# An encoder's second attention layer: five gate tiles instead of seven ahead of the first head group, three behind its operands, and values two token tiles to a PSUM bank

## The chip, the cores and the metric

One core of one Trainium2 chip runs the whole kernel in one launch. The metric is device microseconds of that core. A profiled execution of the same program gives the trace that all rows below come from; its times are counted from the first instruction.

## The reference, cut to what matters

A trunk of two layers over 512 tokens of width 1024. The first layer is a neighbourhood attention and is left alone by the change. The second is a multi-head latent attention of 16 heads, with low-rank queries (384) and keys and values (256), a rotary part of 32 per head, a part of 64 without rotation and values of 64. A gate silu(z) from the same input multiplies its output.

```python
def mixer_mla(xn, w_in, q_norm, w_qb, kv_norm, w_kvb, w_out):
    c_q, c_kv, k_rope, z = split(xn @ w_in, [384, 640, 672])
    q = (rmsnorm(c_q, q_norm) @ w_qb).reshape(B, S, H, 96)
    q_nope, q_pe = split(q, [64]);  q_pe = apply_rope(q_pe, cos, sin)
    kv = (rmsnorm(c_kv, kv_norm) @ w_kvb).reshape(B, S, H, 128)
    k_nope, v = split(kv, [64])
    k_pe = apply_rope(k_rope[:, :, None, :], cos, sin)      # one for all heads
    o = block_attention(concat(q_nope, q_pe), concat(k_nope, k_pe), v)
    return (o.reshape(B, S, H * 64) * silu(z)) @ w_out

for i in range(2):
    xn = rmsnorm(x, norm_g[i])
    h = x + (mixer_na if i == 0 else mixer_mla)(xn, ...)
    gate = sigmoid(rmsnorm(h, ple_norm[i]) @ ple_w_gate[i])
    x = h + gate * (p[i] @ ple_w_proj[i])
return rmsnorm(x, final_norm)
```

## The kernel before, in words

**Numbers.** Every float32 operand of a matmul is held as two tiles, a high part that TensorE takes directly and a low part with what the high part leaves out. A product is three matmuls: high by high, high by low, low by high. For a weight (`load_w`, L67) a DMA on SP brings `wraw`, ScalarE (ACT) copies it to `whi` (L76) and GpSimd (POOL) subtracts to `wlo` (L77). What comes out of PSUM is split in the same way (`split`, L81): ACT copies the high part (L83), VectorE (DVE) subtracts the low one (L85, or L87 with a scale). There are three buffers each of `wraw`, `whi` and `wlo`. PSUM has two banks under the tag `mm` for projections, two under `S` for scores, three under `T` for transposes and one under `O` for a head's output. A bank is 128 partitions by 512 float32.

**Order.** No order of instructions is written by hand across engines. A scheduler goes through the program at build time with a timeline of its own and sets, for each engine and for SP's queue, one fixed order; at run time each engine works its list from top to bottom and waits on semaphores. A tile that takes over a buffer waits until the last reader of the old one is done. `issue_after(i)` tells the scheduler to place nothing of the block ahead of instruction i.

**The second layer.** `mla_c` (L408) projects the layer's input (`x1h`, `x1l`, high and low) to c_q, c_kv and the rotary key, normalises each of four token tiles, rotates the key, transposes to columns (`cT`, high and low, L122) and collects the rotated keys in `slab_h` and `slab_l`. Twelve DMAs on SP (`move`, L89) copy these slabs into two sets of operand tiles: `qe`, `qo`, `ke`, `ko`, the queries and keys of the even and the odd head of a pair, each high and low.

`mla_heads` (L455) does the rest. It first issues the loads of the two rope tables, `rope_c` and `rope_s` (L459, L460). Eight z tiles of 128 gate columns follow one from the other: `z_phase` (L144) loads a weight, runs 24 matmuls of 512 columns into one `mm` bank and has ACT write silu of it to a `z` tile (L152). Seven of them (`NEARLY`, L30) are in the program before the first group, the eighth behind the first projection.

A `group(g)` (L477) serves two pairs, that is four heads: the rotary queries of all four (`psr`, 9 matmuls, copied to `xr` by ACT), the swap of halves `sw` (DVE, L484), the multiplications by the tables (L485 on DVE, L486 on POOL), their sum (L487, POOL), and its split into `rh` (ACT, L490) and `rl`; then the values of four token tiles, six matmuls of 256 columns each into a bank of their own, split by `v_split` (L174) into a tile `vt`; then the load of the weights for the part without rotation. `project(j)` (L507) makes the operands of pair j: nine matmuls for the queries and four evictions out of that bank, six for the keys and four more, and eight small moves of the rotary queries. `attend(j)` (L527) runs the two heads of a pair in `mla_head` (L547): for each of four query tiles three matmuls of scores in a bank `S`, the row maximum (DVE), the exponential `ex` with its sum (ACT), the reciprocal (DVE), the product (POOL), four transposes, the split into `pt_hi` (ACT) and `pt_lo` (DVE); then eight matmuls into the bank `O`. `combine` and `gated` (L157, L166) bring the two heads together in `u`, multiply by the pair's z tile and split into `oT`, whose four tiles are allocated ahead of `mla_heads` (L672). The loop at L535 to L545 strings these together.

## Time and profile before

| what | value |
|---|---|
| time, median of 3 runs | 691.67 us (691.35 to 691.88) |
| the profiled execution's own time | 690.26 us |
| its span, first to last instruction | 688.5 us |
| mean granted TensorE clock | 0.998 |
| first layer and `mla_c`, 0 to 402 | PE busy 391.7 of 402.0 us |
| `mla_heads`, 402 to 585 | PE busy 177.0, ACT 138.4, DVE 132.4, POOL 131.4 of 183.0 us |
| output projection and gate, 585 to the end | PE busy 95.7, POOL 49.4, ACT 42.6, DVE 38.3 of 103.5 us |
| HBM | 65.34 MB read, 8.39 MB written, 107 GB/s over the span |

PE is the TensorE matmul, PEld its weight load, which runs beside it, SP the engine that issues the DMAs. The borders 402 and 585 lie at the last transposes of `mla_c` and behind the last pair's attention. A granted clock of 1.00 is full speed. The busy time of PE is modelled at its ends, so that two waits that lie between back-to-back matmuls can be read better from starts of matmuls than from sums of busy time.

### The profile page before, as it was taken

Reading aid. Unit: us, or ns where it says so; the run is one execution under the profiler, and the core shown is the slowest. Engines: PE = TensorE matmul, PEld = TensorE weight load, DVE = VectorE, ACT = ScalarE, POOL = GpSimd, SP = SyncE. Lnnn points to the kernel's source line nnn. Section 1 sums busy time; section 2 is a strip of 40 time slices with the busy share of each in tenths; the row PEclk is TensorE's granted clock in tenths of the full one; section 3 lists DMA queues with packets and bytes.
Section 4 is the critical chain, followed back from the end, with each engine's and each line's share of the span. In section 5 each row is a group of like instructions: output and inputs, shape, how many; then the busy total and the mean of one; then the engine's idle time right before and its main releaser. Section 6 shows DMA issues by size and latency. Waiting matters only on the chain.

```text
span 688.5 us, 10118 instructions
## 1 busy us (share of the span) xinstructions
PE 664.4 (97%) x3580; PEld 566.9 (82%) x3580; DVE 356.3 (52%) x813; ACT 402.1 (58%) x799; POOL 396.7 (58%) x309
## 2 busy tenths in 40 slices
PE   5999999999999999999999998999999999999995
PEld 4789898998988888788899886787888777887885
DVE  4300364647737624633524503788988886055333
ACT  6722576666767562643443634878888878426433
POOL 1753557467575565853044634777789867658511
PEclk9999999999999999999999999999999999999999
DMA  8731423323223127544243344203121201584122
GB/s 324 234 121 62 133 86 104 105 72 97 85 92 108 40 97 301 167 130 135 89 104 107 107 121 116 81 23 93 24 70 37 86 1 68 191 308 154 61 77 92
DMA packets 28642, 77.53 MB, mean 113 GB/s; under 512 B 3632, under 2 KB 6704, under 8 KB 28592
## 3 DMA queue, kind: packets, MB, share of 16 engines
q1 hardware_dynamic: 28592, 76.89, 33.9%
q8 instruction: 28, 0.46, 0.3%
q14 instruction: 22, 0.18, 0.1%
HBM read 65.34 MB, written 8.39 MB: 107 GB/s over the span
## 4 chain that ended last, share of the span: by engine, by line
PE 86%; ACT 5%; DVE 4%; issue 2%; DMA 1%; POOL 1%; SPq 0%; POOLq 0%; DVEq 0%; ACTq 0%
PE ps_mm L96 63%; PE ps_S L96 9%; PE ps_T L122 5%; PE ps_O L96 4%; PE ps_O L335 2%; PE ps_T L323 1%; ACT ex L561 1%; ACT whi L76 1%; DMA x<-x 1%; PE ps_S L288 1%; PE ps_S L287 1%; DVE mx L559 1%; POOL wlo L77 0%; DVE mx L301 0%; ACT pt_hi L83 0%
## 5 line engine op out<-in xcount | busy, mean ns | idle before, releaser
L77 POOL TENSOR_TENSOR wlo<-wraw,whi 128x1024 fp32r<-128x1024 f32 (+3 forms) x96 | 218.3, 2287 | 118.5 <-ACT whi L76 68.4
L76 ACT ACTIVATE whi<-wraw 128x1024 fp32r<-128x1024 f32 (+4 forms) x100 | 97.9, 988 | 97.0 <-PE ps_mm L96 32.1
L563 POOL TENSOR_TENSOR ex<-ex,rc 128x512 f32<-128x512 f32 x64 | 66.2, 1048 | 20.7 <-DVE rc L562 13.9
L96 PE MATMUL ps_mm<-whi,hnT 128*128 128x512 f32 (+1 forms) x272 | 69.7, 377 | 0.0
L96 PEld LDWEIGHTS ps_mm<-whi,hnT 128*128 128x128 f32 x272 | 49.5, 188 | 9.5
L310 POOL TENSOR_TENSOR ex<-ex,rc 128x128 f32<-128x128 f32 (+1 forms) x64 | 34.3, 560 | 38.1 <-DVE rc L306 36.5
L559 DVE TENSOR_REDUCE mx<-ps_S 128x1 f32<-128x512 f32 x64 | 43.7, 685 | 15.3 <-PE ps_S L96 14.3
L96 PE MATMUL ps_mm<-xh,whi 128*128 128x512 f32 x192 | 50.9, 398 | 0.1
L96 PE MATMUL ps_mm<-xh,wlo 128*128 128x512 f32 x192 | 49.1, 391 | 0.0
L561 ACT ACTIVATE ex<-ps_S,mx 128x512 f32<-128x512 f32 x64 | 44.1, 689 | 8.2 <-DVE mx L559 6.7
L96 PE MATMUL ps_mm<-xl,whi 128*128 128x512 f32 x192 | 48.6, 392 | 0.0
L85 DVE TENSOR_TENSOR pt_lo<-ps_T,pt_hi 128x512 fp32r<-128x512 f32 x64 | 43.0, 679 | 5.0 <-ACT pt_hi L83 4.6
L305 ACT ACTIVATE ex<-ex,mx 128x128 f32<-128x128 f32 (+1 forms) x64 | 30.2, 473 | 22.0 <-DVE mx L301 21.6
L106 POOL TENSOR_TENSOR rs<-ss,half 128x1 f32<-128x1 f32 x24 | 13.0, 549 | 50.3 <-DVE ss L105 49.0
L96 PEld LDWEIGHTS ps_mm<-xl,whi 128*128 128x128 f32 x192 | 35.6, 188 | 7.3
L96 PEld LDWEIGHTS ps_mm<-xh,wlo 128*128 128x128 f32 x192 | 35.6, 188 | 7.0
L83 ACT ACTIVATE pt_hi<-ps_T 128x512 fp32r<-128x512 f32 x64 | 37.0, 597 | 7.6 <-PE ps_T L122 7.3
L96 PE MATMUL ps_mm<-wlo,hnT 128*128 128x512 f32 (+1 forms) x136 | 40.6, 379 | 0.0
L96 PEld LDWEIGHTS ps_mm<-xh,whi 128*128 128x128 f32 x192 | 34.5, 188 | 6.4 <-ACT z L152 0.4
L122 PE MATMUL ps_T<-ident,ex 128*128 128x128 f32 x256 | 36.3, 273 | 0.2 <-DVE pt_lo L85 0.2
L122 PEld LDWEIGHTS ps_T<-ident,ex 128*128 128x128 f32 x256 | 30.7, 141 | 6.8 <-issue 0.7
L85 DVE TENSOR_TENSOR vt<-ps_mm,vt 128x256 fp32r<-128x256 f32 x32 | 13.2, 415 | 44.3 <-ACT vt L83 44.0
(215 smaller groups left out, 1579.7 us busy)
## 6 DMA issues: line engine op xcount, KB each, us to landing
pe<-pe SPq DMA_DIRECT2D x32, 256.0 KB, 2.9
wraw<-na_qk SPq DMA_DIRECT2D x16, 512.0 KB, 3.4
wraw<-gate SPq DMA_DIRECT2D x16, 512.0 KB, 3.4
wraw<-na_z SPq DMA_DIRECT2D x8, 512.0 KB, 4.2
wraw<-na_v SPq DMA_DIRECT2D x8, 512.0 KB, 3.3
wraw<-na_o SPq DMA_DIRECT2D x8, 512.0 KB, 3.4
wraw<-mla_z SPq DMA_DIRECT2D x8, 512.0 KB, 4.2
wraw<-mla_o SPq DMA_DIRECT2D x8, 512.0 KB, 3.6
```

The costliest lines, as they stand in the source:

```text
L76: nc.scalar.activation(hi[:, c], raw[:, c], AF.Copy)
L77: (rest or nc.gpsimd).tensor_tensor(out=lo[:, c], in0=raw[:, c], in1=hi[:, c].bitcast(F32), op=ALU.subtract)
L83: nc.scalar.activation(hi, src, AF.Copy, scale=scale)
L85: nc.vector.tensor_tensor(out=lo, in0=src, in1=hi.bitcast(F32), op=ALU.subtract)
L96: last = nc.tensor.matmul(out, l, r, start=i == 0, stop=i == n - 1)
L122: self.nc.tensor.transpose(t[:, i * P:(i + 1) * P], b, self.ident)
L305: self.last_exp = nc.scalar.activation(e, e, AF.Exp, bias=mx[:, qt:qt + 1], accum_out=sm[:, qt:qt + 1])
L310: nc.gpsimd.tensor_tensor(out=e, in0=e, in1=rc[:, qt:qt + 1].to_broadcast([P, e.shape[1]]), op=ALU.mult)
L335: nc.tensor.matmul(O[:, o:o + w], vh[kt], s[:, c:c + w], start=n == 0, stop=n == 7, skip_group_check=True)
L559: nc.vector.reduce_max(mx[:, c], sp, axis=AX.X, negate=True)
L561: nc.scalar.activation(ex, sp, AF.Exp, bias=mx[:, c], accum_out=sm[:, c])
L563: nc.gpsimd.tensor_tensor(out=ex, in0=ex, in1=rc[:, c].to_broadcast([P, S]), op=ALU.mult)
```

## The change

Five things change, all in the second layer.

1. Five z tiles instead of seven (`NEARLY`) stand in the program ahead of the first group. The sixth comes behind `project(0)`. `attend(0)` may not be placed ahead of its last matmul (`last_mm`), and the seventh and eighth stand behind `attend(0)`.
2. These three are copied raw out of PSUM by DVE. Their silu are then done in place on ACT, the eighth first, each behind the one before it.
3. The values of two token tiles share a bank: twelve matmuls of 256 columns into the two halves, then one split of 512 columns into a `vt` tile of twice the width. There are four such tiles instead of eight.
4. The key-value weights and the weights of the queries without rotation are loaded, copied and split in two halves.
5. The second half of `oT` is allocated in the loop before `attend(3)` rather than at the start.

```diff
-NEARLY = 7
+NEARLY = 5
...
-            last = nc.tensor.matmul(out, l, r, start=i == 0, stop=i == n - 1)
+            last = self.last_mm = nc.tensor.matmul(out, l, r, start=i == 0, stop=i == n - 1)
...
-    def z_phase(self, wap, xT, js, after=None):
+    def z_phase(self, wap, xT, js, after=None, raw=False):
...
             z = self.zp.tile([P, S], F32, name="z", tag="z")
+            zs[j] = z
+            if raw:
+                self.nc.vector.tensor_copy(z, ps)
+                continue
             with self.tc.issue_after(after) if after is not None else nullcontext():
                 self.nc.scalar.activation(z, ps, AF.Silu)
-            zs[j] = z
...
-        src = ps.rearrange("p (g e c) -> p g e c", g=2, e=2)
-        hi = win(vt, 0, P, 0, [[256, 2], [192, 2], [1, 64]])
-        lo = win(vt, 0, P, 64, [[256, 2], [64, 2], [1, 64]])
+        g = ps.shape[1] // 128
+        src = ps.rearrange("p (g e c) -> p g e c", g=g, e=2)
+        hi = win(vt, 0, P, 0, [[256, g], [192, 2], [1, 64]])
+        lo = win(vt, 0, P, 64, [[256, g], [64, 2], [1, 64]])
...
-            wkv = self.load_w(a["mla_kv"][g], 1024)
+            wkv = self.load_w(a["mla_kv"][g], 1024, parts=2)
             vts = []
-            for t in range(NT):
+            for t0 in range(0, NT, 2):
                 ps = self.psum("mm")
...
-                self.mms(ps[:, :256], [(L(0, k), W(0, k)) for k in range(2)] + [(L(1, k), W(0, k)) for k in range(2)]
-                         + [(L(0, k), W(1, k)) for k in range(2)])
-                vt = pool.tile([P, S], F32R, name="vt", tag="vt", bufs=8)
-                self.v_split(vt, ps[:, :256])
-                vts.append(vt)
+                for t in (t0, t0 + 1):
...
+                    self.mms(ps[:, (t - t0) * 256:(t - t0 + 1) * 256],
+                             [(L(0, k), W(0, k)) for k in range(2)] + [(L(1, k), W(0, k)) for k in range(2)]
+                             + [(L(0, k), W(1, k)) for k in range(2)])
+                vt = pool.tile([P, 2 * S], F32R, name="vt", tag="vt", bufs=4)
+                self.v_split(vt, ps)
+                vts += [vt[:, :S], vt[:, S:]]
             V[g] = vts
-            W_[g] = wkv, self.load_w(a["mla_qn"][g], 768)
+            W_[g] = wkv, self.load_w(a["mla_qn"][g], 768, parts=2)
...
-        zs.update(self.z_phase(a["mla_z"], xT, range(NEARLY, 8)))
+        zs.update(self.z_phase(a["mla_z"], xT, [NEARLY], raw=True))
+        first = self.last_mm.ins
         for j in range(8):
             if j < 7 and j % 2 == 1:
                 group((j + 1) // 2)
-            attend(j)
+            if j == 3:
+                for s, n in enumerate("hl"):
+                    oT[s].append(self.bigtile(f"o1{n}1"))
+            with self.tc.issue_after(first) if j == 0 else nullcontext():
+                attend(j)
+            if j == 0:
+                zs.update(self.z_phase(a["mla_z"], xT, range(NEARLY + 1, 8), raw=True))
+                prev = None
+                for i in range(7, NEARLY - 1, -1):
+                    with self.tc.issue_after(prev) if prev is not None else nullcontext():
+                        prev = nc.scalar.activation(zs[i], zs[i], AF.Silu).ins
...
-                oT = ([self.bigtile(f"o1h{g}") for g in range(2)], [self.bigtile(f"o1l{g}") for g in range(2)])
+                oT = ([self.bigtile("o1h0")], [self.bigtile("o1l0")])
```

**The places where the order moves.** The first is the end of `mla_c` on PE, before the change. `ident,cn` are the transposes of the last token tile, `x1h` and `x1l` with a weight are z tiles.

```order
L122 MATMUL ps_T<-ident,cn 128x128 x6
L96 MATMUL ps_mm<-x1h_3092,wlo 128x512 x3
L96 MATMUL ps_mm<-x1h_3093,wlo 128x512 x4
L96 MATMUL ps_mm<-x1h_3092,whi 128x512 x4
L96 MATMUL ps_mm<-x1h_3093,whi 128x512 x4
L96 MATMUL ps_mm<-x1l_3094,whi 128x512 x4
L96 MATMUL ps_mm<-x1l_3095,whi 128x512 x4
```

The same place after the change; `cT` with a weight of 512 columns is the rotary projection of `group(0)`, with one of 256 columns its values.

```order
L122 MATMUL ps_T<-ident,cn 128x128 x6
L96 MATMUL ps_mm<-x1h_3092,wlo 128x512 x3
L96 MATMUL ps_mm<-x1h_3093,wlo 128x512 x4
L96 MATMUL ps_mm<-cT_3484,whi 128x512 x3
L96 MATMUL ps_mm<-cT_3485,whi 128x512 x3
L96 MATMUL ps_mm<-cT_3484,wlo 128x512 x3
L96 MATMUL ps_mm<-whi,cT_3484 128x256 x2
```

Where two z tiles stood behind the end of the z tile that surrounds the transposes, the first group now follows at once.

SP's queue at the same time, before the change, from the last move out of a slab to the first move of a rotary query:

```order
L90 DMA qo_3497<-slab_l 32x512
L75 DMA wraw<-mla_z 128x1024
L75 DMA wraw<-mla_qr 128x384
L459 DMA rope_c<-rope_c 128x512
L460 DMA rope_s<-rope_s 128x512
L75 DMA wraw<-mla_kv 128x1024
L75 DMA wraw<-mla_qn 128x768
L90 DMA qe_3486<-rh 32x512
```

And after it:

```order
L90 DMA qo_3497<-slab_l 32x512
L75 DMA wraw<-mla_z 128x1024
L75 DMA wraw<-mla_qr 128x384
L464 DMA rope_c<-rope_c 128x512
L465 DMA rope_s<-rope_s 128x512
L90 DMA qe_3486<-rh 32x512
```

The loads of the group's value and query weights have gone to places ahead of the moves; the two tables stand where they stood, behind all twelve moves.

The second place is DVE in `group(0)` and `project(0)`, before the change (`qe_3487`, `qo_3489`, `ke_3491`: low parts of the first pair's operands):

```order
L484 STREAM_SHUFFLE sw<-xr 128x512
L85 TENSOR_TENSOR vt<-ps_mm,vt 128x2x128
L485 TENSOR_TENSOR xr<-xr,rope_c 128x512
L85 TENSOR_TENSOR vt<-ps_mm,vt 128x2x128 x3
L87 SCALAR_TENSOR_TENSOR qe_3487<-ps_mm,qe_3486 64x512
L85 TENSOR_TENSOR ke_3491<-ps_mm,ke_3490 64x512
L87 SCALAR_TENSOR_TENSOR qo_3489<-ps_mm,qo_3488 64x512
```

After it:

```order
L489 STREAM_SHUFFLE sw<-xr 128x512
L85 TENSOR_TENSOR vt<-ps_mm,vt 128x4x128
L490 TENSOR_TENSOR xr<-xr,rope_c 128x512
L85 TENSOR_TENSOR vt<-ps_mm,vt 128x4x128
L87 SCALAR_TENSOR_TENSOR qe_3487<-ps_mm,qe_3486 64x512
L85 TENSOR_TENSOR ke_3491<-ps_mm,ke_3490 64x512
L87 SCALAR_TENSOR_TENSOR qo_3489<-ps_mm,qo_3488 64x512
L85 TENSOR_TENSOR ko_3493<-ps_mm,ko_3492 64x512
L154 COPY z<-ps_mm 128x512
```

Four splits of values have become two, one on either side of the multiplication by `rope_c`, and the raw copy of the sixth z tile stands behind the operands.

The third place is ACT. Before the change, from the last high parts of the first pair's operands to the start of its exponentials:

```order
L83 ACTIVATE ko_3492<-ps_mm 64x512
L76 ACTIVATE whi<-wraw 128x384
L152 ACTIVATE z<-ps_mm 128x512
L561 ACT_TABLE_LOAD
L561 ACTIVATE ex,sm<-ps_S,mx 128x512 x2
```

After it, in the second head of the first pair (`u` is the first head's output, `qe_3494` and `qo_3496` belong to the second pair):

```order
L579 ACTIVATE ex,sm<-ps_S,mx 128x512
L76 ACTIVATE whi<-wraw 128x512
L560 ACT_TABLE_LOAD
L560 ACTIVATE z<-z 128x512 x3
L76 ACTIVATE whi<-wraw 128x512
L83 ACTIVATE qe_3494<-ps_mm 64x512
L579 ACT_TABLE_LOAD
L579 ACTIVATE ex,sm<-ps_S,mx 128x512
L164 ACTIVATE u<-ps_O 64x512
L83 ACTIVATE pt_hi<-ps_T 128x4x128
L76 ACTIVATE whi<-wraw 128x384 x2
L83 ACTIVATE qo_3496<-ps_mm 64x512
```

Three silu with a table load on either side have come between two exponentials, where one silu with one table load stood ahead of the first.

2 lines of the change are left out of this document (1 added, 1 removed).

## The prediction, made before the changed kernel was run

> **What bounds the kernel now.** I read the page first, engine lines and then the chain that ended last.
>
> ```profile
> PE 664.4 (97%) x3580; PEld 566.9 (82%) x3580; DVE 356.3 (52%) x813; ACT 402.1 (58%) x799; POOL 396.7 (58%) x309
> PE 86%; ACT 5%; DVE 4%; issue 2%; DMA 1%; POOL 1%; SPq 0%; POOLq 0%; DVEq 0%; ACTq 0%
> ```
>
> TensorE is busy for 664.4 us of a span of 688.5, and 86% of the last chain is matmul. The change takes no matmul away, so it can only win idle time of PE, 24 us in all, or add to it. Where that idle time lies in the second layer is in the table by stretches (stretch; us of PE, PEld, DVE, ACT, POOL; clock; DMA):
>
> ```profile
> 402.00:412.90 10.90, 10.90 (x50) 9.03 (x49) 0.29 (x1) 3.38 (x5) 3.40 (x2) 1.00 0.57 149
> 412.90:425.60 12.70, 10.77 (x53) 7.96 (x52) 5.75 (x11) 6.56 (x12) 8.47 (x5) 1.00 0.53 148
> 425.60:438.80 13.20, 11.87 (x55) 9.69 (x55) 4.73 (x10) 7.88 (x15) 5.48 (x5) 1.00 0.12 35
> 438.80:468.80 30.00, 28.86 (x159) 24.23 (x159) 25.63 (x52) 24.08 (x55) 22.45 (x19) 1.00 0.19 52
> 468.80:585.00 116.20, 114.61 (x616) 94.46 (x617) 96.00 (x197) 96.53 (x212) 91.56 (x78) 1.00 0.18 55
> ```
>
> From 402.0 to 412.9 PE works through two z tiles without a pause. It idles 1.9 us in the first group and projection, 1.3 us at the start of the attention, 1.1 us more by 468.8 and 1.6 us in the whole remaining 116 us. So about 6 us are there to be won.
>
> **What the change moves: the first group to an earlier time.** Five z tiles instead of seven stand ahead of group(0). The timeline of PE at its borders (start, us, line, operands, count):
>
> ```profile
> 399.81 0.82 PE L122 MATMUL ps_T<-ident,cn 128*128 128x128 f32 x6
> 402.08 1.98 PE L96 MATMUL ps_mm<-x1h,whi 128*128 128x512 f32 x8
> 412.96 1.52 PE L96 MATMUL ps_mm<-cT,whi 128*128 128x512 f32 x6
> 425.64 2.06 PE L96 MATMUL ps_mm<-x1h,whi 128*128 128x512 f32 x8
> 82.82 5.47 PE ps_mm L96 x24
> ```
>
> The last row is a piece of the chain: 24 matmuls of 512 columns take 5.47 us when they run back to back, 0.228 us each. That is a z tile. Before, the sixth z tile begins at 402.08, group(0) at 412.96 and the eighth z tile at 425.64. After the change the same transposes (399.81) are followed by group(0) at 402.1, 10.9 us earlier, because everything ahead of it on PE stands as it did.
>
> What group(0) needs does not all move with it. Its rotation multiplies by the rope tables, and these stand in SP's queue behind the twelve moves out of slab_h and slab_l, in the old program and in the new one. SP's timeline, and from the views of both table tiles the time to landing:
>
> ```profile
> 402.30 0.60 SPq L90 DMA_DIRECT2D ke<-slab_h  x1
> 409.30 0.59 SPq L90 DMA_DIRECT2D qo<-slab_l  x1
> 411.07 1.50 SPq L459 DMA_DIRECT2D rope_c<-rope_c  x1
> 412.62 0.42 SPq L460 DMA_DIRECT2D rope_s<-rope_s  x1
> ...
> DMA to landing us min/median/max: 4.5/4.5/4.5
> ...
> DMA to landing us min/median/max: 3.6/3.6/3.6
> ```
>
> The moves start when the last slab_h is written and take SP until 409.9 (first and last of twelve shown). rope_c lands at 411.07 + 4.5 = 415.6, rope_s at 416.2. Before, that was just early enough:
>
> ```profile
> 402.00 0.28 ACT L83 ACTIVATE slab_h<-ps_T 128x128 fp32r<-128x128 f32 x1 [0.79 <-DVE cT L85]
> 402.28 0.60 ACT L152 ACTIVATE z<-ps_mm 128x512 f32<-128x512 f32 x1
> 416.15 0.76 DVE L484 STREAM_SHUFFLE sw<-xr 128x512 f32<-128x512 f32 x1
> 417.12 1.52 DVE L485 TENSOR_TENSOR xr<-xr,rope_c 128x512 f32<-128x512 f32 x1
> 418.05 1.73 POOL L486 TENSOR_TENSOR sw<-sw,rope_s 128x512 f32<-128x512 f32 x1
> 419.86 1.29 POOL L487 TENSOR_TENSOR xr<-xr,sw 128x512 f32<-128x512 f32 x1
> 421.18 0.63 ACT L490 ACTIVATE rh<-xr 128x512 fp32r<-128x512 f32 x1 [0.70 <-POOL xr L487]
> 422.10 0.59 ACT L83 ACTIVATE qe<-ps_mm 64x512 fp32r<-64x512 f32 x1 [0.29 <-PE ps_mm L96]
> 422.72 0.68 DVE L87 SCALAR_TENSOR_TENSOR qe<-ps_mm,qe 64x512 fp32r<-64x512 f32 x1 [1.79 <-ACT qe L83]
> 424.80 0.69 DVE L87 SCALAR_TENSOR_TENSOR qo<-ps_mm,qo 64x512 fp32r<-64x512 f32 x1
> ```
>
> The multiply by rope_c ran at 417.12 with 1.5 us to spare. With group(0) at 402.1, its rotary projection ends nine matmuls later at 404.1, and DVE has shuffled it by about 406. The table is not there for ten more microseconds. It is even a little later, since ACT now evicts z (0.60, not before 402.28) ahead of the last slab_h: slab_h is done at 403.1 instead of 402.3, the moves start 0.8 us later, and rope_c lands at 416.4, rope_s at 417.0.
>
> What is queued behind that wait decides the price. On DVE, in the new order, the multiply stands ahead of the low half of the second value pair. The key projection needs the PSUM bank of that pair, so PE stops after the query projection. That is 18 matmuls of 512 columns (4.1 us) and 24 of 256 (half of that each, an estimate: 2.7 us) after 402.1, so at about 409. The multiply takes 1.5 us (417.9), the low half of a 512-column tile about 0.68 us, and PE goes on at 418.6, after some 9.5 us of nothing. On ACT, rh stands ahead of the evictions of the queries: sw on POOL 417.0 to 418.5 (1.3 to 1.7), the add 1.29 to 419.8, rh 0.63 to 420.4, qe 0.59 to 421.0, then on DVE the low halves of qe, ke and qo, 0.68 + 0.68 + 0.69, to 423.1. The sixth z tile takes the bank of the queries, and in the new PE order all scores wait behind that tile. It starts at 423.1.
>
> Now the sum against the old timeline. At 425.64 the old kernel had done the same work and besides two z tiles (10.94 us) and four score matmuls (0.91 us). So the new one is behind by 423.1 + 10.94 + 0.91 - 425.64 = **9.3 us**. The old waits inside the first group (0.3 and 0.8 us in the 1.9) are in this difference already. Bounds, taking the shortest and longest multiply (0.8 and 1.6) and sw (1.3 and 1.7): 8.6 to 9.9.
>
> **The clock.** An idle PE loses its clock here. Around the last matmul, which ends at 681.0, the stretches show:
>
> ```profile
> 681.00:685.00 4.00, 0.03 (x1) 0.00 (x0) 1.93 (x6) 1.71 (x4) 1.23 (x2) 1.00 0.29 110
> 685.80:688.00 2.20, 0.00 (x0) 0.00 (x0) 0.00 (x0) 0.00 (x0) 0.00 (x0) 0.50 0.53 197
> ```
>
> After less than 4.8 us without matmuls the granted clock is 0.50. A gap of 9.5 us is twice as long. At the program's start matmuls of this width come 0.43 us apart for the first 3 us:
>
> ```profile
> 8.62 0.63 PE L96 MATMUL ps_mm<-wlo,whi 128*128 128x512 f32 x1
> 9.05 0.63 PE L96 MATMUL ps_mm<-whi 128*128 128x512 f32 x1
> 9.84 0.40 PE L96 MATMUL ps_mm<-wlo,whi 128*128 128x512 f32 x1
> 10.08 0.39 PE L96 MATMUL ps_mm<-whi 128*128 128x512 f32 x1
> ```
>
> The key projection's six matmuls at that pace last 2.6 us instead of 1.4, to 421.2, and this hides behind rh. The z tile then pays between nothing and 3 us at half pace, 1.5 us. I take 1.0; bounds 0 to 2.7. The Trainium skill (TensorE: Matmul & The Clock Gate, What's actually happening) says that the array falls to half clock after an idle window of about 3.4 us and regains it after about 3.4 us of work. The rows here agree, and by that figure the term would be 1.7 us.
>
> **Silu in one go.** ACT's new order sets, between the third and fourth exponential of the first pair's second head, half of a weight copy, a table load, three silu, the other half, the eviction of qe and a second table load. Durations:
>
> ```profile
> 431.37 0.60 ACT L152 ACTIVATE z<-ps_mm 128x512 f32<-128x512 f32 x1 [1.24 <-PE ps_mm L96]
> 431.98 1.28 ACT L561 ACT_TABLE_LOAD   x1
> 433.28 0.69 ACT L561 ACTIVATE ex<-ps_S,mx 128x512 f32<-128x512 f32 x1
> 436.04 0.84 ACT L76 ACTIVATE whi<-wraw 128x768 fp32r<-128x768 f32 x1
> 438.83 0.96 PE L96 MATMUL ps_S<-ko,qo 128*128 128x512 f32 x3 [1.32 <-ACT ex L561]
> L563 POOL TENSOR_TENSOR ex<-ex,rc 128x512 f32<-128x512 f32 x64 | 66.2, 1048 | 20.7 <-DVE rc L562 13.9
> ```
>
> Two loads 2.56, three silu 1.7 (they overlap by 0.1), two halves 1.1 and qe 0.6: 6 us. Then come the exponential 0.7 with its sum 0.2, a reciprocal 0.2 and POOL's 1.05, so 8 us until PE can turn that tile. PE has, behind the score matmuls that the tile needs, the rest of the query projection (2 matmuls), 8 of the first output, 8 transposes and 6 of the key projection: 16 x 0.228 plus 8 x 0.11 (0.82 for 6, pipelined), 4.5 us. It waits about 3. Next it needs ke of the second pair, for which ACT first does u, one pt_hi, two weight halves and qo, some 3.3 us after the exponential: another 1.4 us of waiting. Against these 4.4 us stands the old wait of 1.32 us before the second head, which the z tiles now cover: net **+2.9 us**. Bounds: -1.5 (ACT reaches the silu in a lull) to +4.4. The Trainium skill (ScalarE: Activation LUTs, What ACT_TABLE_LOAD costs) counts 2.66 us for a switch, with a drain behind the load. The rows disagree: z, the load and the next exponential follow one another within 1.9 us. By the page the term would be 2.8 us larger; the rows decide.
>
> **What lies beside other work.** The three raw copies (DVE, near 0.68 each) run while PE works on the next tile. Two evictions of 512 columns instead of four of 256, and weight halves instead of whole copies, change ACT, DVE and POOL by well under 1 us a group; if that cover were gone, at most 1 us for each of three later groups. The later pairs keep their work in another order; they idle 1.6 us over 116, so I allow -1.6 to +3 and take 0. The tiles that are allocated later only free buffers.
>
> Sum: 9.3 + 1.0 + 2.9 = 13.2 us on the profiled execution's 690.26. The median of the runs, 691.67, stands 1.4 us above that execution; the same step gives **704.9**.
>
> **Rivals.**
> - The cover works: the change does what its words say, and PE fills the first pair's latencies with z tiles. It wins the waits at 412.9 to 438.8 (1.9 + 1.3) and part of the 1.1 behind them, about -4: 687.5. This decides if the rope tables are there by about 407; for it speaks only that nothing in the order says when a DMA starts, and against it the moves' 0.6 us each on SP.
> - The rope wait alone: the clock stays up or hides, and the silu fall into a lull. 9.3 - 1.5 to 9.3 + 1: 699.5 to 702.
> - Worse: after the gap ACT stays late, and each later pair pays again, say 1.3 us (the size of the old wait) for four pairs on top: 710 and more.
> - Slower by less: half of the gap is spared because SP starts its moves earlier, +3 to +5: 695 to 697.
>
> **Chances.** Forecast (702 to 709): 0.66. Rope wait alone (698 to 702): 0.16. Worse (over 709): 0.07. Slower by less (693 to 698): 0.05. Cover works or nothing changes: 0.06. The first two with the edges of their neighbours give 697.5 to 710, which is about what the bounds give: 8.6 + 0 - 1.5 - 1.6 = +5.5, and +18 with three of the four terms at their upper end. Faster by over 0.2% (1.4 us, about what a measurement of this kernel can tell from no change) 0.04, within 0.03, slower 0.93.
>
> **What would show it.** The multiply by rope_c on DVE with some 10 us of idle time before it, released by the DMA; one PE gap of 9 us released by DVE's vt; a clock of 0.50 in the rows around 415 to 424; a second gap of about 2 us before the sixth z tile; two waits of 3 and 1.4 us behind ACT some 30 us later. It is wrong if rope_c is issued before 405, or if PE's gap ends on something other than that multiply.

## The result and the profile after

The changed kernel takes 712.94 us (median of 4 runs, 711.8 to 714.42) against 691.51 for the kernel before: a ratio of 1.0311, 95% interval 1.0291 to 1.0331. It is 21 us slower, 8 us more than forecast and 2.9 us above the range, which ended at 710. The profiled execution took 714.42 us, the slowest of the four; its span is 712.6 us, 24.2 more than before's, at a mean granted clock of 0.979.

The page of the changed kernel: TensorE's busy time, its granted clock in 40 slices, and the chain that ended last by engine.

```profile
PE 673.7 (95%) x3580; PEld 573.1 (80%) x3580; DVE 357.4 (50%) x808; ACT 406.7 (57%) x801; POOL 397.3 (56%) x317
PEclk9999999999999999999999959989999999999999
PE 81%; ACT 6%; DVE 5%; POOL 2%; DMA 2%; issue 2%; SPq 1%; POOLq 0%; DVEq 0%; ACTq 0%
```

The number of matmuls is the same, yet PE is busy 9.3 us longer, and the clock has dips in the second layer where it had none. (The 40 slices show two, at 5 and at 8; the stretches below show a third, too short for a slice of 17.8 us.) Longer busy time and dips point to one thing: matmuls that run at half pace count as busy. The other part is idle time. PE's own timeline at the last transposes of `mla_c`, 1.3 us later than before, and at its five largest waits in `mla_heads` (start, us, operands, count, idle time ahead of it and what ended it):

```profile
401.11 0.81 PE L122 MATMUL ps_T<-ident,cn 128*128 128x128 f32 x6
...
418.73 2.07 PE L96 MATMUL ps_mm<-cT,whi 128*128 128x512 f32 x4 [7.97 <-DVE vt L85]
424.08 1.19 PE L96 MATMUL ps_mm<-x1h,whi 128*128 128x512 f32 x2 [2.43 <-DVE qo L87]
...
460.66 0.92 PE L122 MATMUL ps_T<-ident,ex 128*128 128x128 f32 x4 [3.09 <-POOL ex L581]
462.64 1.22 PE L96 MATMUL ps_S<-ke,qe 96*128 96x512 f32 x2 [1.06 <-ACT ke L83]
...
565.78 0.63 PE L122 MATMUL ps_T<-ident,ex 128*128 128x128 f32 x4 [1.96 <-DVE pt_lo L85]
```

The first four waits are those of the prediction: the key projection at 418.7, the sixth z tile at 424.1, and two waits of 3 and 1 us behind ACT. What ends the first lies one step back, on DVE, ACT and SP of the same kernel:

```profile
413.13 0.42 SPq L464 DMA_DIRECT2D rope_c<-rope_c  x1
...
417.39 0.69 DVE L490 TENSOR_TENSOR xr<-xr,rope_c 128x512 f32<-128x512 f32 x1 [9.02 <-DMA rope_c<-rope_c]
418.00 0.68 DVE L85 TENSOR_TENSOR vt<-ps_mm,vt 128x512 fp32r<-128x512 f32 x1
...
413.46 0.60 ACT L83 ACTIVATE vt<-ps_mm 128x512 fp32r<-128x512 f32 x1 [5.82 <-DMA qo<-slab_l]
```

DVE waits 9.0 us for the table and then frees the bank that PE wants. ACT's row shows a second wait under the first: its copy of the second value pair waited 5.8 us for the last move out of a slab, since the new `vt` tile lies in memory that the slab still held. The prediction didn't have it; with the table's wait on top it cost nothing.

ACT around the silu in one go:

```profile
453.23 1.28 ACT L560 ACT_TABLE_LOAD   x1
454.52 1.67 ACT L560 ACTIVATE z<-z 128x512 f32<-128x512 f32 x3
...
457.22 1.28 ACT L579 ACT_TABLE_LOAD   x1
458.52 0.69 ACT L579 ACTIVATE ex<-ps_S,mx 128x512 f32<-128x512 f32 x1
```

From the first load to the exponential pass 5.3 us, and PE waits for that exponential's product at 460.66.

The clock, in stretches with borders where it changed (stretch; us of PE, PEld, DVE, ACT, POOL; clock; DMA share, GB/s):

```profile
409.71:413.13 3.42, 1.05 (x5) 0.54 (x3) 0.00 (x0) 0.00 (x0) 0.00 (x0) 1.00 0.60 136
413.13:430.19 17.06, 9.03 (x20) 6.62 (x21) 3.87 (x6) 3.37 (x6) 3.81 (x3) 0.50 0.32 100
457.50:460.91 3.41, 0.32 (x3) 0.25 (x3) 1.55 (x4) 3.35 (x7) 1.61 (x2) 1.00 0.49 152
460.91:467.74 6.83, 5.77 (x16) 4.30 (x15) 3.62 (x6) 3.71 (x9) 1.95 (x2) 0.50 0.18 58
563.31:566.73 3.42, 1.46 (x10) 0.96 (x9) 3.42 (x6) 3.42 (x9) 3.42 (x3) 1.00 0.02 8
566.73:570.14 3.41, 3.41 (x12) 2.72 (x11) 3.20 (x9) 2.65 (x6) 2.90 (x4) 0.50 0.60 195
```

Half clock lasts 17.06, 6.83 and 3.41 us: five, two and one times 3.41. Each time the 3.41 us ahead of it are a stretch in which PE was busy for under half. The loss is half of what PE did there: the sixth z tile ran at half clock from 424.08 to 430.19, 3.05 us lost; 5.77 at the second dip, 2.9 lost; 3.41 at the third, 1.7 lost. That is 7.65 us. (The first dip also slowed the key projection, which hides behind `rh`.)

And the later pairs, before in one row and after in the other, from the first pair's end to the last one's:

```profile
440.00:590.00 150.00, 147.29 (x794) 121.88 (x793) 120.48 (x246) 120.41 (x266) 112.80 (x96) 1.00 0.20 60
```

```profile
467.74:605.00 137.26, 131.46 (x700) 108.18 (x700) 109.20 (x219) 110.24 (x239) 104.03 (x92) 0.99 0.16 46
```

PE idled 2.7 us there before and 5.8 us after.

### The profile page after: what moved, and what is told of

It is laid out like the page before. It is cut to its first block, busy times and chain, and to the rows that moved or that the text cites. A ratio compares the mean times of both kernels' runs of the same rounds, so it can differ in the third digit from the quotient of the medians.

```text
span 712.6 us, 10117 instructions
## 1 busy us (share of the span) xinstructions
PE 673.7 (95%) x3580; PEld 573.1 (80%) x3580; DVE 357.4 (50%) x808; ACT 406.7 (57%) x801; POOL 397.3 (56%) x317
## 4 chain that ended last, share of the span: by engine, by line
PE 81%; ACT 6%; DVE 5%; POOL 2%; DMA 2%; issue 2%; SPq 1%; POOLq 0%; DVEq 0%; ACTq 0%
PE ps_mm L96 60%; PE ps_S L96 8%; PE ps_T L122 4%; PE ps_O L96 3%; PE ps_O L340 2%; PE ps_T L328 1%; ACT ex L579 1%; DMA x<-x 1%; PE ps_S L293 1%; PE ps_S L292 1%; POOL wlo L77 1%; DVE mx L577 1%; SPq L90 1%; DVE pt_lo L85 1%; ACT whi L76 1%
## 5 line engine op out<-in xcount | busy, mean ns | idle before, releaser
L77 POOL TENSOR_TENSOR wlo<-wraw,whi 128x1024 fp32r<-128x1024 f32 (+4 forms) x104 | 219.7, 2127 | 119.0 <-ACT whi L76 73.3
L577 DVE TENSOR_REDUCE mx<-ps_S 128x1 f32<-128x512 f32 x64 | 43.8, 685 | 14.9 <-PE ps_S L96 14.6
L122 PE MATMUL ps_T<-ident,ex 128*128 128x128 f32 x256 | 38.6, 277 | 5.1 <-POOL ex L581 3.1
L96 PE MATMUL ps_mm<-cT,whi 128*128 128x512 f32 x104 | 31.0, 428 | 8.4 <-DVE vt L85 8.0
```

What stands on the lines that cost most here:

```text
L77: (rest or nc.gpsimd).tensor_tensor(out=lo[:, c], in0=raw[:, c], in1=hi[:, c].bitcast(F32), op=ALU.subtract)
L96: last = self.last_mm = nc.tensor.matmul(out, l, r, start=i == 0, stop=i == n - 1)
L122: self.nc.tensor.transpose(t[:, i * P:(i + 1) * P], b, self.ident)
L577: nc.vector.reduce_max(mx[:, c], sp, axis=AX.X, negate=True)
```

## The experiments

Theory 1 is the prediction's: the wait for the rope tables, the silu in one go and the clock make the loss. The main rival, called rival 2 below, is that values pair and weight halves, costed at nothing, carry part of it. Ratios are to the kernel before, timed on the same chip.

| run | what | median us | ratio (95%) |
|---|---|---|---|
| e1 | change, rope tables early | 708.16 | 1.0243 (1.0228 to 1.0259) |
| e8 | e1, slabs in other memory | 702.62 | 1.0163 (1.0142 to 1.0185) |
| e2 | change without the three silu | 703.87 | 1.0179 (1.0164 to 1.0195) |
| e9 | change, PE kept busy in two gaps | 710.91 | 1.0285 (1.0270 to 1.0300) |
| e3 | z move alone | 706.46 | 1.0220 (1.0203 to 1.0237) |
| e4 | values pair, halves, late oT | 696.23 | 1.0071 (1.0056 to 1.0086) |
| e5 | values pair alone | 696.74 | 1.0083 (1.0068 to 1.0098) |
| e6 | halves alone | 695.41 | 1.0057 (1.0042 to 1.0072) |
| e7 | late oT alone | 691.35 | 0.9999 (0.9989 to 1.0008) |
| e12 | halves of the copies alone | 694.14 | 1.0044 (1.0029 to 1.0058) |
| e13 | e5 with a bank of the scores | 695.19 | 1.0053 (1.0040 to 1.0066) |
| e14 | z move alone with e8's edits | 695.64 | 1.0060 (1.0047 to 1.0073) |
| e10 | one z tile between | 693.75 | 1.0027 (1.0014 to 1.0040) |
| e11 | eighth z tile moved | 691.40 | 1.0003 (0.9994 to 1.0011) |
| e15 | e10 with free banks | 690.96 | 0.9993 (0.9983 to 1.0003) |
| e16 | e15 with one more | 686.70 | 0.9946 (0.9933 to 0.9960) |

**e1: the rope tables loaded early.**

```diff
 def mla_c(...):
         nc.sync.dma_start(tok, a["rope_tok"])
+        for t, n in zip(self.rope, ("rope_c", "rope_s")):
+            nc.sync.dma_start(t, a[n])
...
 def run(...):
+                self.rope = [pool.tile([P, S], F32, name=n, tag=n, bufs=1) for n in ("rope_c", "rope_s")]
                 with tc.tile_pool(name="mlac", bufs=2, reuse_waits="tile") as cpool:
...
 def mla_heads(...):
-        rc_t = pool.tile([P, S], F32, name="rope_c", tag="rope_c", bufs=1)
-        rs_t = pool.tile([P, S], F32, name="rope_s", tag="rope_s", bufs=1)
-        nc.sync.dma_start(rc_t, a["rope_c"])
-        nc.sync.dma_start(rs_t, a["rope_s"])
+        rc_t, rs_t = self.rope
```

> The changed kernel with the two rope tables loaded at the start of mla_c, ahead of the slab moves; nothing else differs. Theory 1 (the tables behind the moves are the first wait): the multiply by rope_c runs at about 408.5 instead of 417.4, and the next thing late is ACT's copy of the second value pair, which waited for the last slab move to land (413.4) because vt takes the slabs' memory. PE's first gap ends at about 415 instead of 418.7, the second (before the sixth z tile) shrinks from 2.4 to 1.5 us or less; the gap of 4 us still costs the clock. Time 706 to 709, against 712.9. Rival (the tables are not what ends the wait): 711 to 714.

It came out at 708.16 us, as Theory 1 had it, 4.8 us below the change. In its trace the multiply runs at 408.2; PE's and ACT's timelines show what is late instead:

```profile
414.84 2.07 PE L96 MATMUL ps_mm<-cT,whi 128*128 128x512 f32 x4 [4.21 <-DVE vt L85]
...
413.47 0.60 ACT L83 ACTIVATE vt<-ps_mm 128x512 fp32r<-128x512 f32 x1 [5.95 <-DMA qo<-slab_l]
```

The wait for the slab moves is now the outer one, and PE's gap is 4.2 us where it was 8.0.

**e8: the slabs in the z pool as well.**

```diff
-        slab_h = pool.tile([P, S], F32R, name="slab_h", tag="slab", bufs=2)
-        slab_l = pool.tile([P, S], F32R, name="slab_l", tag="slab", bufs=2)
+        slab_h = self.zp.tile([P, S], F32, name="slab_h", tag="z")[:, :].bitcast(F32R)
+        slab_l = self.zp.tile([P, S], F32, name="slab_l", tag="z")[:, :].bitcast(F32R)
```

> The changed kernel with the rope tables loaded early, as in the first run, and the two slabs in buffers of the z pool, so that the values' tiles no longer wait for the slab moves to land. Theory 1: the gap of 4.2 us before the key projection goes to under 1; rh (at about 411.5) and the evictions of the queries behind it on ACT then set the sixth z tile at about 414.5, a gap of some 3.5 us behind the key projection. Later waits stay. 704 to 707, against 708.2 with the early tables alone. Rival (the moves are not what the second value pair waits for): 708, as without it.

702.62 us, better than expected. PE's timeline, the query projection and the sixth z tile:

```profile
408.61 1.66 PE L96 MATMUL ps_mm<-cT,whi 128*128 128x512 f32 x6 [1.29 <-DVE vt L85]
...
414.52 3.52 PE L96 MATMUL ps_mm<-x1h,whi 128*128 128x512 f32 x8 [2.21 <-DVE qo L87]
```

The gap before the key projection is gone. The z tile starts at 414.5, as expected, behind a gap of 2.2 us instead of 3.5, since a wait of 1.3 us now stands before the query projection. The expectation had left out how the clock would come back: one stretch of 3.41 us at half was left where e1 had three. Both waits together, tables and slab, are worth 10.3 us.

**e2: no silu in one go.** The silu of z tiles six to eight is left out.

```diff
-                prev = None
-                for i in range(7, NEARLY - 1, -1):
-                    with self.tc.issue_after(prev) if prev is not None else nullcontext():
-                        prev = nc.scalar.activation(zs[i], zs[i], AF.Silu).ins
```

> The changed kernel without the silu of the last three z tiles (the gate of their heads is left without it) and so without the two table loads around them. Theory 1: the waits of 3.1 and 1.1 us at 460.7 and 462.6 go, and with them the half clock from 460.9 to 467.7 (about 2.9 us): 705 to 707. Rival (these waits belong to the second pair's weights and operands, which come late anyway): under 2 us, 711 or more.

703.87 us: 9.1 us less, and more than expected. The stretch behind the first head in its trace:

```profile
439.70:475.00 35.30, 35.30 (x190) 29.77 (x189) 25.48 (x49) 25.00 (x54) 24.67 (x22) 1.00 0.21 62
```

PE has no pause there and full clock. Besides the 4.2 us of waits and 2.9 us of clock, the third dip (1.7 us) was gone too: ACT's order in the later pairs is another one without the silu, and where the changed kernel had one wait of 1.96 us this run has two of 0.96 and 0.56.

**e9: PE kept busy.** Matmuls that nobody reads, in the gaps; the z tile is held behind the second lot.

```diff
+            if j == 0:
+                with self.tc.issue_after(self.last_mm.ins):
+                    d = self.psum("O")
+                    for i in range(33):
+                        w = nc.tensor.matmul(d, ch[:, i % 3, 0:P], ch[:, i % 3, :], start=True, stop=True)
             psk = self.psum("mm")
-            last = kproj(psk, wkv, jj * 256)
+            with self.tc.issue_after(w.ins) if j == 0 else nullcontext():
+                last = kproj(psk, wkv, jj * 256)
...
```

> The changed kernel with matmuls that nobody reads put into its first two gaps of PE: 33 of 512 columns between the query and the key projection, 11 between the key projection and the sixth z tile. The waits for the rope tables and for the evictions stay as they are; only PE is not idle in them. If the clock is the mis-sized term: the granted clock stays 1.00 until the third gap at about 460, the sixth z tile starts near 424 as before but takes 5.5 us where it took 8.6, and the time falls by 3 to 4 us to 708.5 to 710. If the clock costs nothing beyond the waits: 712 to 714.5.

710.91 us, 2.0 less than the change and between the two expectations; the runs just overlap (709.52 to 712.54 against 711.80 to 714.42). PE's timeline in this run (L531 and L538 are the added matmuls):

```profile
409.89 7.65 PE L531 MATMUL ps_O<-cT 128*128 128x512 f32 x33
419.35 1.42 PE L96 MATMUL ps_mm<-cT,whi 128*128 128x512 f32 x4 [1.80 <-DVE vt L85]
...
421.42 3.70 PE L538 MATMUL ps_O<-cT 128*128 128x512 f32 x11
424.95 1.98 PE L96 MATMUL ps_mm<-x1h,whi 128*128 128x512 f32 x8
```

The sixth z tile goes at full pace (8 matmuls in 1.98 us; in e8's row above 8 took 3.52). The gain fell short of 3 to 4 us because a pause of 1.8 us remained behind the 33, one stretch of 3.41 us still ran at half, and the second lot held the z tile back to 424.95. With the waits left as they are and PE busy in them, the five stretches at half clock became one: that PE's idle time takes the clock away is shown by the trace; the exact 3.05 us are not.

**e3 and e4: the change in two halves.** e3 has the z move with values and weights as before; e4 has values pair, halves and late `oT` with the z tiles as before.

```diff
e3, against the changed kernel:
-            wkv = self.load_w(a["mla_kv"][g], 1024, parts=2)
+            wkv = self.load_w(a["mla_kv"][g], 1024)
-            for t0 in range(0, NT, 2):
+            for t in range(NT):
...
-            W_[g] = wkv, self.load_w(a["mla_qn"][g], 768, parts=2)
+            W_[g] = wkv, self.load_w(a["mla_qn"][g], 768)
e4, against the changed kernel:
-NEARLY = 5
+NEARLY = 7
...
-        zs.update(self.z_phase(a["mla_z"], xT, [NEARLY], raw=True))
+        zs.update(self.z_phase(a["mla_z"], xT, range(NEARLY, 8)))
...
```

> The changed kernel with the values one token tile to a bank and the weights whole, as before; the z tiles, their raw copies and the silu in one go stay. Theory 1 (all of the loss is the move of the z tiles; what exceeded the forecast is the clock): 711 to 715, as the whole change. Rival 2 (the 3.4 us of waits in later pairs come from the wider value splits and the halves, which were costed at nothing): 706 to 709.

> The kernel before with the values two token tiles to a bank, the weights in halves and the late half of oT, but seven z tiles ahead and direct silu as before. Theory 1: 690.5 to 692.5, no change. Rival 2: 694 to 696.

Both went to the rival: 706.46 us, and 696.23, just above its range. The z move alone costs 14.9 us. That this is close to the 13.2 of its three terms is partly chance: in e3's trace the half clock around the silu alone costs 3.0 us, and the later pairs idle less than before. (That trace is of the fastest of four runs, 704.28 us at a mean clock of 0.989; the others had 0.983 and 0.984.) The other parts cost 4.6 us by themselves and 6.5 on top of it. The later pairs in e3 and in e4:

```profile
464.00:597.00 133.00, 131.47 (x713) 109.35 (x713) 110.55 (x226) 111.69 (x245) 104.47 (x89) 1.00 0.17 51
```

```profile
443.00:594.00 151.00, 145.78 (x780) 119.25 (x779) 118.58 (x239) 119.86 (x261) 113.01 (x100) 1.00 0.18 55
```

PE idles 1.5 us in e3, less than the 2.7 before, and 5.2 in e4. The extra waits of the later pairs come with values and halves.

**e5, e6, e7: those parts one by one,** on the kernel before.

```diff
e5: group() and v_split() of the changed kernel, with load_w(..., 1024) and load_w(..., 768) whole
e6:
-            wkv = self.load_w(a["mla_kv"][g], 1024)
+            wkv = self.load_w(a["mla_kv"][g], 1024, parts=2)
-            W_[g] = wkv, self.load_w(a["mla_qn"][g], 768)
+            W_[g] = wkv, self.load_w(a["mla_qn"][g], 768, parts=2)
e7:
-                oT = ([self.bigtile(f"o1h{g}") for g in range(2)], [self.bigtile(f"o1l{g}") for g in range(2)])
+                oT = ([self.bigtile("o1h0")], [self.bigtile("o1l0")])
+            if j == 3:
+                for s, n in enumerate("hl"):
+                    oT[s].append(self.bigtile(f"o1{n}1"))
```

> The kernel before with the values two token tiles to a bank, and nothing else of the change. The run with values, halves and late oT lost 4.6 us. Theory A (the pair: both banks are held until twelve matmuls and a 512-column split are through, so the query projection waits for one whole split behind the multiply, and the operands of the first pair come later): 694 to 696. Theory B (it is one of the two others): 691 to 692.

> The kernel before with the key-value and query weights loaded, copied and split in halves, and nothing else of the change. Theory A: 691 to 692. Theory B1 (two ACT copies and two POOL subtractions instead of one each cost ACT, in the attention where it is busy 27 of 30 us, its slack): 693 to 696.

> The kernel before with the second half of oT allocated before attend(3), and nothing else of the change. The scheduler has two more large buffers for pt_hi and pt_lo until then, so its order may move. Theory A: 690.5 to 692. Theory B2 (the other order gives back slack in the early pairs and takes it in later ones): 693 to 696.

The pair costs 5.3 us (696.74, above the range of Theory A), the halves 3.9 (695.41, as B1 had it), the late `oT` nothing (691.35); pair and halves together (e4) cost no more than one of them, and why they don't add up stays open. Pair first, then halves: the later pairs.

```profile
443.00:594.00 151.00, 146.66 (x786) 120.29 (x786) 119.28 (x240) 120.84 (x260) 113.34 (x96) 1.00 0.19 58
```

```profile
441.00:591.00 150.00, 145.21 (x783) 119.75 (x782) 120.89 (x246) 121.01 (x269) 112.88 (x100) 1.00 0.19 56
```

Idle 4.3 and 4.8 us, against 2.7. ACT's busy time is nearly what it was (120.8 of 151 and 121.0 of 150 us, before 120.4; it is not the 27 of 30 us that e6's expectation gives). In e6 the added waits go with other places in line: up to 477 us ACT's list differs from before only by halves in the place of whole copies, and PE idles 0.2 us more from 440 on; behind that ACT, DVE and PE work in another order, and PE idles 1.9 us more. The groups of score matmuls show these waits, before and then in e6 (busy, mean ns, idle time ahead of them and what ended it):

```profile
L96 PE MATMUL ps_S<-ke,qe 96*128 96x512 f32 x92 | 27.4, 407 | 1.4 <-ACT ex L561 1.4
```

```profile
L96 PE MATMUL ps_S<-ke,qe 96*128 96x512 f32 x92 | 27.4, 409 | 3.5 <-ACT ex L561 3.2
```

They wait 1.8 us longer for an exponential.

Four runs of the halves show the clock as a step: 693.70 us at a mean clock of 0.997, and 695.12, 695.71 and 695.74 at 0.994, 1.4 to 2.0 us apart, about one stretch of 3.41 us at half. So about 2 of the 3.9 us are waits, and the rest is that step. The pair pays at the start too. PE's timeline of e5:

```profile
420.84 1.65 PE L96 MATMUL ps_mm<-cT,whi 128*128 128x512 f32 x6 [1.43 <-DVE vt L85]
...
426.42 0.93 PE L96 MATMUL ps_S<-ke,qe 96*128 96x512 f32 x3 [1.89 <-DMA qe<-rh]
```

3.3 us in two waits, and a stretch of half clock behind the second, where before had 0.8 and 0.7 without one.

**e12: which half of the halves.** Weights loaded whole, copied and subtracted in halves; ACT's order is e6's.

```diff
...
+        if whole:
+            nc.sync.dma_start(raw[:, :n], ap)
         for c in [slice(i * w, (i + 1) * w) for i in range(parts)]:
-            nc.sync.dma_start(raw[:, c], ap[:, c])
+            if not whole:
+                nc.sync.dma_start(raw[:, c], ap[:, c])
...
```

> The kernel before with the key-value and query weights loaded whole, as before, but copied on ACT and subtracted on POOL in halves. ACT's order is the one of the run with halves alone. If the 3.9 us of the halves come from the copies and the order that they make: 694.5 to 696 again. If they come from the halved loads (the second half lands later): 691 to 692.

694.14 us: slower than before without any halved load, just under the expected range. The later pairs idle as in e6, within 0.01 us:

```profile
441.00:591.00 150.00, 145.22 (x783) 119.84 (x782) 121.28 (x246) 121.55 (x270) 113.38 (x100) 1.00 0.18 56
```

So the later pairs' waits come from the copies and the order that they make, not from the loads; 2.6 of the 3.9 us are shown so. One more instruction and the other order weren't told apart by a run; that most of the waits lie where the order differs speaks for the order.

**e13: does the pair cost by the banks it holds?** The second pair of `group(0)` in a bank of the scores.

```diff
-                ps = self.psum("mm")
+                ps = self.psum("S" if g == 0 and t0 else "mm")
```

> The kernel with the values pair alone, and group(0)'s second pair in a bank of the scores, which is free at that time. If the held banks are what the pair costs at the start: PE's wait of 1.43 us before the query projection goes, the wait of 1.89 before the scores and the half clock behind it go or shrink, 692.5 to 694.5 against 696.7. The waits in the later pairs (7.3 us by the pair's trace, 5.2 before) stay. Rival (the pair's cost is all in the later pairs' order): 696 to 697.

695.19 us, 1.55 less than e5 and between the two expectations. The wait before the query projection went, but the one before the scores grew from 1.89 to 2.64 us, still for a move of the rotary queries: half of the time came back one step later. Yet no clock was lost there. The stretches around that wait:

```profile
420.83:424.24 3.41, 1.57 (x7) 0.95 (x6) 1.56 (x4) 2.36 (x5) 2.59 (x3) 1.00 0.25 91
424.24:427.66 3.42, 2.62 (x12) 2.21 (x13) 1.25 (x2) 0.53 (x1) 0.04 (x1) 1.00 0.46 108
```

The border of the stretches at 424.24 cuts the gap in two. A pause of 2.64 us was free of it, where the one of 1.96 us in the changed kernel was not. Half clock came later in this trace, in the pairs, behind two pauses of 0.52 and 1.27 us. e5 has the same two pauses at the same matmuls without it. The stretches around them, in e13 and then in e5:

```profile
543.66:547.07 3.41, 1.62 (x6) 0.97 (x6) 2.50 (x6) 3.14 (x7) 3.41 (x3) 1.00 0.50 168
547.07:550.48 3.41, 3.41 (x9) 2.65 (x8) 3.27 (x5) 1.60 (x4) 3.41 (x4) 0.50 0.45 156
```

```profile
544.10:547.51 3.41, 2.89 (x15) 2.11 (x14) 2.54 (x6) 2.92 (x7) 3.41 (x4) 1.00 0.40 118
547.51:550.92 3.41, 2.14 (x9) 1.44 (x9) 2.44 (x6) 3.31 (x7) 3.41 (x3) 1.00 0.25 75
```

In e13 both pauses fall into one stretch; in e5 a border parts them.

**e14: do the parts add up?** e3 with the edits of e1 and e8.

> The z move alone (values and halves as before), with the rope tables early and the slabs in the z pool. If the parts add up: 706.5 less the 10.3 us that both edits took off the whole change, 695 to 698, with the silu's waits of 3.0 and 0.8 us at about 450 and their half clock still there. If they don't (values and halves are what made the tables' wait dear): 699 or more.

695.64 us, 10.8 below e3: they add up. What is left of the z move is the wait for the queries' bank (2.2 us) and the silu with their waits and half clock.

**e10, e11: can covering win?** Both start from the kernel before, with direct silu. e10 has the tables and slabs of e8, six z tiles ahead, one between `group(0)` and `project(0)`, one behind; e11 only moves the eighth between them.

```diff
e10:
-NEARLY = 7
+NEARLY = 6
...
         group(0)
+        zs.update(self.z_phase(a["mla_z"], xT, range(NEARLY, NEARLY + 1)))
         last = project(0)
-        zs.update(self.z_phase(a["mla_z"], xT, range(NEARLY, 8)))
+        zs.update(self.z_phase(a["mla_z"], xT, range(NEARLY + 1, 8)))
+        first = self.last_mm.ins
...
-            attend(j)
+            with self.tc.issue_after(first) if j == 0 else nullcontext():
+                attend(j)
e11:
         group(0)
+        zs.update(self.z_phase(a["mla_z"], xT, range(NEARLY, NEARLY + 1)))
         last = project(0)
-        zs.update(self.z_phase(a["mla_z"], xT, range(NEARLY, 8)))
```

> The kernel before with the idea of the change but not its form: the rope tables loaded early, the slabs in the z pool, six z tiles ahead, the seventh between group(0) and project(0), the eighth behind project(0), and attend(0) held until its last matmul; silu straight out of PSUM, values, weights and oT as before. The z tile behind group(0) covers the rotary chain, the one behind project(0) the evictions. If covering works when its operands are there: the waits of 0.95 and 0.84 us in group(0) and project(0) and the 1.49 before the second head go, 687.5 to 690. Rival (another order in the pairs gives it back): 690.5 to 693.

> The kernel before with one thing changed: the eighth z tile stands between group(0) and project(0) rather than behind it, and seven are ahead as before. If a z tile covers the rotary chain: the wait of 0.95 us for the values' bank goes, the wait of 0.84 before the scores and what follows stay: 689.5 to 691. Rival (the tile is missed behind the first scores, where it now covers the exponentials, and PE waits there for up to 2 us): 692 to 694.

Neither won. e10 is 0.27% slower; PE's timeline at its last z tile says why:

```profile
425.53 0.47 PE L96 MATMUL ps_mm<-x1h,whi 128*128 128x512 f32 x1 [2.21 <-DVE qo L87]
```

The tile that was to cover the evictions waits for them itself: there are two banks for projections, and it needs the queries'. e11 came out even, 691.40 us. Its expectation was wrong on where the tile goes: it stands behind all values, so the wait for their bank (0.79 us) stayed; 691.40 lies between its two expectations.

**e15, e16: give the z tiles banks of their own.** e15 is e10 with the eighth z tile in bank O and the third and fourth value tile of `group(0)` in banks S, all idle at that time; e16 puts the seventh z tile into O too.

```diff
e15:
-            ps = self.psum("mm")
+            ps = self.psum(tag)
...
-                ps = self.psum("mm")
+                ps = self.psum("S" if g == 0 and t >= 2 else "mm")
...
-        zs.update(self.z_phase(a["mla_z"], xT, range(NEARLY + 1, 8)))
+        zs.update(self.z_phase(a["mla_z"], xT, range(NEARLY + 1, 8), tag="O"))
e16, besides:
-        zs.update(self.z_phase(a["mla_z"], xT, range(NEARLY, NEARLY + 1)))
+        zs.update(self.z_phase(a["mla_z"], xT, range(NEARLY, NEARLY + 1), tag="O"))
```

> The run with a z tile between group(0) and project(0), with the eighth z tile in the bank O and the third and fourth value tile of group(0) in the banks of the scores. The wait of 2.2 us for the queries' bank and its half clock, and the 0.8 us for the values' bank, go; the later waits stay as they were there or move. 688.5 to 690.5. Rival (the order in the pairs turns and takes it back): 691 to 693.

> The run before (a z tile between group(0) and project(0), values in the banks of the scores) with the seventh z tile in the bank O too, so that it need not wait for the values' bank. The wait of 1.0 us at 413.9 goes: 689 to 690. Rival (the order in the pairs turns and takes it back): 690.5 to 692.5.

e15 is even with before (690.96 us, half a microsecond above the expected range); one wait for a bank was left:

```profile
413.90 0.50 PE L96 MATMUL ps_mm<-x1h,whi 128*128 128x512 f32 x1 [1.02 <-DVE vt L85]
```

e16 is faster than both kernels: 686.70 us, ratio 0.9946 (0.9933 to 0.9960), more than expected. The start of the heads, before and in e16:

```profile
402.00:440.00 38.00, 34.71 (x162) 27.62 (x161) 11.90 (x23) 19.02 (x34) 18.55 (x12) 1.00 0.40 106
```

```profile
402.00:440.00 38.00, 37.58 (x187) 31.37 (x186) 16.30 (x32) 21.99 (x43) 23.72 (x16) 1.00 0.43 116
```

PE idles 0.4 us where it idled 3.3. The idea of the change holds in this form (six z tiles ahead, one between and one behind), once tables, slab memory and banks are there and no silu stands between exponentials.

## Why the prediction was wrong, by its steps

**The first group: right.** The forecast had PE going on at 418.6 and the sixth z tile at 423.1; they came at 418.73 and 424.08. The whole timeline was 1.3 us later already (the last transposes stand at 401.11, before at 399.81; in the other 16 traces they lie between 399.57 and 400.98), so that by the same comparison the step is 424.08 - 1.3 + 10.94 + 0.91 - 425.64 = 9.0 us, against 9.3. e1 and e8 show that tables and slab make it. What the step had missed is that two waits lay on top of each other, and part of its accuracy is luck: the slabs' wait, which it didn't have, was hidden, and the multiply began 1.0 us later than forecast but took 0.69 us instead of 1.5.

**The clock: the step that failed.** The term was 1.0 us, with 2.7 at most. It was 7.65. The prediction let the clock fall once, behind the longest gap, and let it come back after some 3 us of work, most of it hidden. The trace shows it at half for 17 us there, since the second gap at 421.7 kept it down, and it fell twice more, behind the silu's gap of 3.1 us, which the prediction had priced by its length alone, and behind one of 2.0 us in the later pairs, which it didn't have. e9 shows the mechanism, and e6's four runs the size of one step.

**Silu in one go: right in its waits.** 3 and 1.4 us were forecast, 3.1 and 1.1 measured; less the old 1.32 us that is a net 2.8, against 2.9. Its whole price in e2 is 9.1 us, because the clock goes with it, there (2.9 us) and in the later pairs (1.7).

**What lies beside other work: failed.** "Well under 1 us a group" and 0 for the later pairs were the terms; the range allowed 3. Values pair and halves cost 4.6 us by themselves (e4), and the later pairs idle 3.1 us more, 5.8 against 2.7. The estimate compared durations of instructions. By e6 and e12, what matters is the order that regrouped work takes on ACT and DVE, in a stage where DVE and ACT are each busy for four fifths of the time (120.5 and 120.4 of 150 us, before) and PE has next to no slack; this is argued from the places of the waits, not tested apart. The third dip of the clock lies here too.

The sum on the profiled execution: 9.0 + 7.65 + 2.8 + 3.1 = 22.55 us, with 1.3 us from ahead of the change 23.9 of the 24.2.

**The rivals.** "Worse" has the measured time, but not by its mechanism: without values pair and halves the later pairs idle less than before (e3, e14). "The rope wait alone" fails on the silu, worth 9.1 us in e2, and "slower by less" on SP, which issued `rope_c` at 413.13, not earlier. "The cover works" did not hold for the change; its estimate of 4 us won is about what e16 wins by other means (4.4 us).

## What to carry to other kernels

When a step is moved ahead, list everything it waits for, one under the other (its tables' place in the DMA queue, the memory its tiles take over, its PSUM banks), and move all of them, or the next one takes over part of the price (here 4.2 of 8.0 us). A pause of PE of some 2 us can cost a step of clock besides its length, 1.7 us here, and two short ones close together can too: count each. In a stage where two engines are busy for four fifths and the third has no slack, an edit that only regroups their work can have a price: time it alone before it goes in with others.

## What the runs showed of the hardware

The granted clock is set in stretches of 3.41 us, one behind the other, at places that differ from run to run (half clock sets in at 413.13 us in the changed kernel and, at the same wait, at 414.98 in e2). In the 18 traces of this case there are 3,462 such stretches between 20 and 680 us. At full clock, all 16 in which PE was busy for less than 45% were followed by half clock; of six at 47 or 48% four were and two were not; of those above 50% none was. At half clock, all 16 in which PE was busy 82% of the time or less were followed by half clock again, and all 20 that were full by full clock. So the clock falls after less idle time than one stretch (1.96 us in the changed kernel), and where the stretches' border falls decides whether the same pauses cost 1.7 us more or nothing (e13 and e5). The clock goes with part of the spread of the changed kernel's times: 713.21 and 714.42 us at a mean of 0.979, 711.80 and 712.67 at 0.984. The Trainium skill (TensorE: Matmul & The Clock Gate, What's actually happening) has the window of 3413 ns, free-running, and the trace agrees (3.41 us); where it asks for an idle window, the stretches show that one busy for less than 45% was idle enough in all 16 cases, and one busy for 47 or 48% in four of six.
